# A two-layer encoder trunk on one core: seven-product matmuls over ten instead of eight of the sixteen row blocks

## The chip, the cores and the metric

The kernel runs on one core of a Trainium2 chip, as one program in one launch. The metric is device time in microseconds (us), from the first to the last work of the core; of several runs the median is taken. TensorE does the matmuls, VectorE and ScalarE the element-wise work, GpSimd some element-wise work and some DMA issue, SyncE issues most weight loads. In the profile's rows these are PE (PEld for its weight loads), DVE, ACT, POOL and SP.

## The reference, cut to what matters

256 frames of 2048 float32 features go through two layers. Layer 0 mixes with sparse attention, layer 1 with a convolution module; in both an MLP and a gated embedding follow:

```python
def sq_relu_mlp(hn, w1, w2):          # w1: 2048 x 8192, w2: 8192 x 2048
    a = jax.nn.relu(hn @ w1)
    return (a * a) @ w2
...
h = h + sq_relu_mlp(rmsnorm(h, norm_mlp_g[i]), mlp_w1[i], mlp_w2[i])
h = h + jax.nn.sigmoid(h @ ple_w_gate[i]) * (p[i] @ ple_w_proj[i])
```

The convolution of layer 1 is depthwise with 31 taps per channel. Everything is float32; the output is the normalized h.

## The kernel before

Weights stream from HBM in raw tiles of up to two row blocks (128 rows by 512 columns each, 256 KB a block). Each raw tile is split into two parts, `wh` (a ScalarE copy to the fast matmul format) and `wl` (VectorE: raw minus `wh`), and the activations are split the same way, so each block product takes three matmuls: high by high, high by low, low by high. `halves` does the split; its `wh` and `wl` tiles lie in rings of `SPLITS` buffers, and a buffer comes free when TensorE has used the tile in it.

The MLPs and the gates go through `pair_gemm`, which computes 256 frames by 1024 output columns from 2048 inputs; one call is a **pair** below. There are 36: 16 for each layer's MLP and two for each layer's gates. An MLP is done in four blocks of 2048 hidden columns, each block being four pairs: the first and the second hidden pair (**H1**, **H2**), which end in squared ReLU, transposes and a fresh split into the activations `a`; and the first and second residual pair (**R1**, **R2**), which add to `h`.

Within a pair the first `2 * SP` of the 16 row blocks go through the seven-product scheme (Strassen's, in Winograd's form): the weights of even and odd row blocks and of the two column halves form four sets `a`, `b`, `c`, `d` of `SP` blocks each, the activations are kept as sums of quarters (`Sums`), and seven products of `SP` blocks do the work of eight. `seven(m, ...)` is product m; they stand in the order 0, 5, 3, 4, 1, 6, 2. Between them the weights are summed in place: `b` is added to `a`, and later to `d`, by a DMA that accumulates (issued from GpSimd); `d` and then `c` are added to `a` on VectorE (`add`). A block of a seven-product set serves one of the two frame halves at a time, so its split feeds 3 matmuls. The other `16 - 2 * SP` row blocks are plain (`plain`): the split of a plain block feeds both frame halves, 6 matmuls.

The four results x, y, v, z gather in four PSUM banks; `taken` evicts them, early parts through ScalarE copies (hidden pairs) or VectorE adds (residual pairs), final parts through VectorE. `Sums.put` turns two transposed blocks into the sums that the seven products need (ScalarE copies, VectorE differences, two splits); plain blocks need only a split.

All raw tiles share one ring of `RAWS` = 9 tiles. Small closures are put off by steps (`defer`, `step`), and a scheduling pass of the compiler then orders each engine's instructions. Each engine takes its own in that order, and those that wait hold up what stands behind them.

The convolution's taps `wdw` are loaded and transposed (`taps`) while layer 0's attention output is projected; `wdl` holds a second, low set of taps for two channel tiles.

Of the kernel before, what the change touches and what calls it, by code (L numbers as in the profile page):

```python
# [17 lines left out]
P = 128  # L18
# [34 lines left out]
SP = 4  # L53
# [5 lines left out]
SPLITS = 6  # L59
# [3 lines left out]
def encoder(ctx: ExitStack, tc: tile.TileContext, A, inv_freq, out):  # L63
# [101 lines left out]
    class Sums:  # L165
# [19 lines left out]
        def put(self, kk, pt, g=None):  # L185

            if kk >= 2 * SP:
                h, l = (v[:, kk - 2 * SP:kk - 2 * SP + 2, :] for v in self.rest)
                put_blocks((h, l), pt, None if g is None else g[:, kk:kk + 2])
                return  # L190
            y, z, v = work(4, P), work(4, P), work(2, P)
            for k, dst in ((0, v), (1, z[:, 1:3, :])):
                nc.scalar.activation(dst, pt[:, k], AF.Copy, scale=g[:, kk + k:kk + k + 1] if g is not None else 1.0)
            x11, x21, x12, x22 = v[:, 0, :], v[:, 1, :], z[:, 1, :], z[:, 2, :]
            tt = nc.vector.tensor_tensor
            nc.vector.tensor_scalar(y[:, 0, :], x11, -1.0, None, op0=ALU.mult)
            tt(y[:, 2, :], x21, x11, op=ALU.subtract)
            tt(y[:, 3, :], x21, x22, op=ALU.subtract)
            tt(y[:, 1, :], x11, y[:, 3, :], op=ALU.subtract)
            tt(z[:, 0, :], x12, y[:, 1, :], op=ALU.subtract)  # L200
            i = kk // 2
            for dst, src in ((self.four, y), (self.more, z[:, :3, :])):
                split(dst[0][:, :, i, :], dst[1][:, :, i, :], src)
# [11 lines left out]
    def pair_gemm(x, src, taken, extras=(), apart=False):  # L215
# [13 lines left out]
        def load(ks, n):  # L229
            raw = raw_tile(len(ks))  # L230
# [21 lines left out]
        def raw(name, q):  # L252
            if (name, q) not in raws:
                raws[name, q] = load(*rows(name, q))
# [19 lines left out]
        def plain(n, ks):  # L274
            step()
            w = halves(load(ks, n))
# [17 lines left out]
        for r in ks[:-2]:  # L294
# [7 lines left out]
        plain(0, ks[-2])  # L302
# [13 lines left out]
    def raw_tile(nk, n=NB):  # L316
        return wpool.tile([P, KG, NB], F32, name="raw", tag="raw", bufs=RAWS)[:, :nk, :n]
# [472 lines left out]
    def ple(layer, x, done, e, pr, last=None):  # L790
# [3 lines left out]
        for ch in range(2):  # L794

            def projections(n, ch=ch):
                w = []

                def project(t):
                    if not w:  # L800
                        r = raw_tile(2)
# [43 lines left out]

    PE_TILES = [p[0] for p in PE_PLAN]
    wdw = const.tile([P, KT, CONV_W + 1], F32, name="wdw")
    wdl = const.tile([P, len(PE_TILES), CONV_W + 1], F32, name="wdl")

    def taps(c):  # L850
        pw = at_tile().rearrange("p (k i) -> p k i", k=KT)
        wr = work(NB)[:CONV_W]
        nc.scalar.dma_start(wr, A["b_w_dw"][0][:, c * NB:(c + 1) * NB])

        def turn():
            for k in range(4):
                nc.tensor.transpose(pw[:, k, :CONV_W], wr[:, k * P:(k + 1) * P], ident[:CONV_W, :CONV_W])
            nc.vector.tensor_copy(wdw[:, 4 * c:4 * c + 4, :CONV_W], pw[:, :4, :CONV_W])
            for i, kk in enumerate(PE_TILES):
                if kk // 4 == c:  # L860
                    wdh = small.tile([P, CONV_W + 1], F32R, name="wdh")
                    nc.scalar.activation(wdh[:, :CONV_W], wdw[:, kk, :CONV_W], AF.Copy)
                    nc.vector.tensor_tensor(wdl[:, i, :CONV_W], wdw[:, kk, :CONV_W], wdh[:, :CONV_W].bitcast(F32),
                                            op=ALU.subtract)
        defer(1, turn)
    for c in range(4):
        defer(12 + 2 * c, lambda c=c: taps(c))

# [12 lines left out]
    with tc.tile_pool(name="cnv", bufs=1) as cnv:  # L881
        u = cnv.tile([P, KT, UW], F32, name="u")
# [4 lines left out]
        class Diagonals:  # L887

            def __init__(self, kk, where):
                self.kk, self.done = kk, 0
                flat = lambda v: v.rearrange("p k s -> p (k s)").rearrange("p (i j) -> p i j", j=P)
                if where == "hl":
                    hi, lo = xpair("A")
                    m = PE_TILES.index(kk)
                    self.sets = [(flat(hi), wdw[:, kk]), (flat(lo), wdl[:, m])]
                else:
                    self.sets = [(flat(acts.tile([P, KT, S], F32, name="dg", tag=f"x{where}A")), wdw[:, kk])]
                self.some()  # L900

            def some(self, n=BUILD):
                with tc.issue_after(recent[0]):
                    for i in range(self.done, min(self.done + n, CONV_W)):
                        for d, w in self.sets:
                            nc.scalar.activation(d[:, i, :], ident, AF.Copy, scale=w[:, i:i + 1])
# [6 lines left out]
        def conv_pe(kk):  # L913
# [5 lines left out]
            if len(d.sets) == 1:  # L919
                for i in range(CONV_W):  # L920
                    nc.tensor.matmul(acc, d.sets[0][0][:, i, :], u[:, kk, i:i + S], start=i == 0, stop=i == CONV_W - 1)
            else:
                uh = cnv.tile([P, UW], F32R, name="uh")
                ul = cnv.tile([P, UW], F32R, name="ul")
                split(uh, ul, u[:, kk, :])
                hi, lo = d.sets[0][0], d.sets[1][0]
                for i in range(CONV_W):
                    nc.tensor.matmul(acc, hi[:, i, :], uh[:, i:i + S], start=i == 0, stop=False)
                    nc.tensor.matmul(acc, lo[:, i, :], uh[:, i:i + S], start=False, stop=False)
                    nc.tensor.matmul(acc, hi[:, i, :], ul[:, i:i + S], start=False, stop=i == CONV_W - 1)  # L930
# [192 lines left out]
```

## Time and profile before

| what | value |
|---|---|
| median of 3 runs | 2248.43 us (2247.61 to 2248.62) |
| profiled execution, its own time | 2248.04 us |
| its span, first to last instruction | 2246.3 us |
| mean granted TensorE clock | 0.998 |
| busy: PE, PEld, DVE, ACT, POOL | 2224.4, 1847.5, 1874.4, 1432.1, 428.6 us |
| chain that ended last, by engine | PE 93%, DVE 4%, issue 1%, DMA 1%, ACT 1% |

The span lies 1.7 us inside the profiled execution's time. Busy time is the time in which an engine has at least one instruction in flight; matmuls overlap, so the pace of TensorE is read from the starts of its matmuls and not from their durations.

### The profile page before, as it was taken

To read this page: it belongs to the slowest core of one execution; us is meant where nothing else is said; L and a number is where in the kernel's file an instruction comes from. 1 tells how busy PE (TensorE), PEld (TensorE's weight loads), DVE (VectorE), ACT (ScalarE), POOL (GpSimd) and SP (SyncE) were. 2 spreads that over 40 slices of the span, in tenths; PEclk is the share of its full clock that TensorE was granted. 3 is DMA by queue.
4 is the path that set the end of the run, shared out by engine and by line. 5 is a ranking of instruction groups with operands and counts; after the bars stand their busy time and mean duration, and the time that the engine had idled before them with its cause. 6 is when DMAs were issued, how large, how long until landed. Compare 5 with 4: busy or idle time off the path is not lost.

```text
span 2246.3 us, 29595 instructions
## 1 busy us (share of the span) xinstructions
PE 2224.4 (99%) x10366; PEld 1847.5 (82%) x10366; DVE 1874.4 (83%) x2516; ACT 1432.1 (64%) x1920; POOL 428.6 (19%) x313
## 2 busy tenths in 40 slices
PE   9999999999999999999999999999999999999998
PEld 7888778888888888888898887888888888888886
DVE  5658657988888888889868999789889889889987
ACT  6545546765765765766765744577567577577675
POOL 0201210111011011011139872111111101101012
PEclk9999999999999999999999999999999999999999
DMA  8655446887887887887767552677877877877884
GB/s 278 198 150 171 148 128 169 224 249 204 234 242 203 238 240 202 243 232 202 205 194 226 181 175 67 201 199 201 275 205 202 271 201 209 270 196 216 237 245 121
DMA packets 268021, 463.42 MB, mean 206 GB/s; under 512 B 16340, under 2 KB 62308, under 8 KB 267744
## 3 DMA queue, kind: packets, MB, share of 16 engines
q1 hardware_dynamic: 225840, 381.88, 50.9%
q0 software_dynamic: 39168, 75.51, 20.1%
q10 hardware_dynamic: 2864, 4.15, 0.6%
q8 instruction: 81, 1.33, 0.2%
q14 instruction: 68, 0.56, 0.1%
HBM read 459.38 MB, written 2.10 MB: 205 GB/s over the span
## 4 chain that ended last, share of the span: by engine, by line
PE 93%; DVE 4%; issue 1%; DMA 1%; ACT 1%; POOL 0%; SPq 0%; POOLq 0%; DVEq 0%; ACTq 0%
PE pm L238 42%; PE at L238 21%; PE pm L347 8%; PE pm L349 8%; PE pm L348 8%; PE pt L763 1%; DVE at L950 1%; PE at L808 1%; DVE wl L323 1%; PE pt L428 1%; PE at L612 0%; PE at L659 0%; PE at L689 0%; DMA work<-in_b_w_dw 0%; DMA raw<-in_a_w_in 0%
## 5 line engine op out<-in xcount | busy, mean ns | idle before, releaser
L322 ACT ACTIVATE wh<-raw 128x1024 fp32r<-128x1024 f32 (+2 forms) x1032 | 1058.8, 1040 | 621.8 <-PE at L238 187.8
L323 DVE TENSOR_TENSOR wl<-raw,wh 128x1024 fp32r<-128x1024 f32 (+1 forms) x955 | 1146.5, 1223 | 267.1 <-ACT wh L322 250.6
L261 POOL DMA_DIRECT2D raw<-in_mlp_w x128 | 155.1, 1212 | 1203.1 <-DVE wl L323 1076.3
L238 PE MATMUL pm<-wl,xhA 128*128 128x512 f32 x504 | 197.7, 392 | 0.0
L238 PE MATMUL pm<-wl,xhB 128*128 128x512 f32 x504 | 197.5, 392 | 0.0
L238 PE MATMUL pm<-wh,xlB 128*128 128x512 f32 x504 | 196.4, 391 | 0.0
L238 PE MATMUL pm<-wh,xlA 128*128 128x512 f32 x504 | 196.4, 391 | 0.0
L238 PE MATMUL pm<-wh,xhB 128*128 128x512 f32 x504 | 192.5, 392 | 0.0
L238 PE MATMUL pm<-wh,xhA 128*128 128x512 f32 x504 | 192.3, 393 | 0.0
L347 PE MATMUL pm<-wh,xhA 128*128 128x512 f32 (+2 forms) x480 | 184.1, 388 | 1.4 <-ACT xhA L382 0.6
L349 PE MATMUL pm<-wh,xlA 128*128 128x512 f32 (+2 forms) x480 | 183.6, 387 | 0.5 <-DVE xlA L1041 0.5
L348 PE MATMUL pm<-wl,xhA 128*128 128x512 f32 (+2 forms) x480 | 183.8, 384 | 0.0
L263 DVE TENSOR_TENSOR raw<-raw 128x1024 f32<-128x1024 f32 x144 | 175.5, 1220 | 1.0
L323 POOL TENSOR_TENSOR wl<-raw,wh 128x1024 fp32r<-128x1024 f32 (+1 forms) x77 | 158.3, 2079 | 30.2 <-ACT wh L322 29.1
L347 PE MATMUL pm<-wh,xhB 128*128 128x512 f32 (+1 forms) x448 | 163.1, 365 | 0.0
L348 PE MATMUL pm<-wl,xhB 128*128 128x512 f32 (+1 forms) x448 | 162.0, 362 | 0.0
L349 PE MATMUL pm<-wh,xlB 128*128 128x512 f32 (+1 forms) x448 | 161.8, 363 | 0.0
L950 DVE SCALAR_TENSOR_TENSOR at<-u,wdw,at 128x256 f32<-128x256 f32 x402 | 160.5, 483 | 0.0
L238 PE MATMUL at<-wh,xlA 128*128 128x512 f32 x360 | 140.9, 391 | 0.0
L238 PE MATMUL at<-wh,xhA 128*128 128x512 f32 x360 | 140.8, 391 | 0.0
L238 PE MATMUL at<-wh,xlB 128*128 128x512 f32 x360 | 140.8, 391 | 0.0
L238 PE MATMUL at<-wh,xhB 128*128 128x512 f32 x360 | 140.7, 391 | 0.0
(228 smaller groups left out, 3951.1 us busy)
## 6 DMA issues: line engine op xcount, KB each, us to landing
raw<-in_mlp_w SPq DMA_DIRECT2D x448, 512.0 KB, 5.4
raw<-in_mlp_w POOLq DMA_DIRECT2D x128, 512.0 KB, 6.4
raw<-in_a_w_in SPq DMA_DIRECT2D x72, 512.0 KB, 4.1
raw<-in_ple_w_gate SPq DMA_DIRECT2D x56, 512.0 KB, 5.6
raw<-in_b_w_pw SPq DMA_DIRECT2D x96, 256.0 KB, 3.1
raw<-in_a_w_out SPq DMA_DIRECT2D x32, 512.0 KB, 3.7
raw<-in_b_w_pw SPq DMA_DIRECT2D x32, 512.0 KB, 4.3
raw<-in_ple_w_gate POOLq DMA_DIRECT2D x16, 512.0 KB, 6.2
```

The source lines that it names most:

```text
L238: nc.tensor.matmul(bank[v], l, r, start=v not in begun, stop=bool(left[v] == 0 or (last and j == 2)), skip_group_check=v in again)
L261: nc.gpsimd.dma_start(r, piece(*rows(other, q)), accum_op=ALU.add)
L263: nc.vector.tensor_tensor(r, r, raw(other, q), op=ALU.add)
L322: recent[0] = nc.scalar.activation(wh, r, AF.Copy).ins
L323: (low or nc.vector).tensor_tensor(wl, r, wh.bitcast(F32), op=ALU.subtract)
L347: nc.tensor.matmul(pm[t][:, :n], a, wh[:, i], start=k + i == 0, stop=False)
L348: nc.tensor.matmul(pm[t][:, :n], a, wl[:, i], start=False, stop=False)
L349: nc.tensor.matmul(pm[t][:, :n], b, wh[:, i], start=False, stop=k + i == kt - 1)
L428: nc.tensor.transpose(pt[:, k, t, :], h[:, t, (kk + k) * P:(kk + k + 1) * P], ident)
L763: nc.tensor.transpose(pt[:, k, t, :], both[t][:, 2 * j + k, :], ident)
L808: nc.tensor.matmul(pp, l, r[:, k], start=k == 0 and j == 0, stop=k == 1 and j == 2)
L950: nc.vector.scalar_tensor_tensor(dst, src, w, z, op0=ALU.mult, op1=ALU.add)
```

## The change

`SP` goes from 4 to 5: the seven products run over ten row blocks and six stay plain. A set of five blocks is held in three raw tiles (one block, two, two) where four blocks were two tiles of two. `SPLITS` goes from 6 to 5. The one raw ring becomes three: tiles of the sets in a ring of 6 (`kept`), single-block tiles of the sets in a ring of 3 of their own, plain tiles in a ring of 3 (`used`); other matmuls take turns between the first and the last. With three plain tiles a column half in place of four, two of the first half stand before product 3 and one after product 2; the one between products 1 and 6 is gone. The sign change in `Sums.put` moves from VectorE to ScalarE where no gain is applied. The second set of taps (`wdl`) is dropped with the code that could use it, and the loading of the taps moves to the first steps of the convolution module.

```diff
-SP = 4
+SP = 5
...
-SPLITS = 6
+USED = 3
+SPLITS = 5
...
-            nc.vector.tensor_scalar(y[:, 0, :], x11, -1.0, None, op0=ALU.mult)
+            if g is None:
+                nc.scalar.activation(y[:, 0, :], pt[:, 0, 0], AF.Copy, scale=-1.0)
+            else:
+                nc.vector.tensor_scalar(y[:, 0, :], x11, -1.0, None, op0=ALU.mult)
...
-                raws[name, q] = load(*rows(name, q))
+                raws[name, q] = load(*rows(name, q), "kept")
...
-            w = halves(load(ks, n))
+            w = halves(load(ks, n, "used"))
...
-        for r in ks[:-2]:
+        for r in ks[:-1]:
             plain(0, r)
         seven(3, "z", "a", part="z1")
         add("a", "d")
...
         seven(1, "x", "a", part="x2")
         add("a", "c")
-        plain(0, ks[-2])
         seven(6, "v", "a")
         seven(2, "x", "d", part="x3")
         plain(0, ks[-1])
...
-    def raw_tile(nk, n=NB):
-        return wpool.tile([P, KG, NB], F32, name="raw", tag="raw", bufs=RAWS)[:, :nk, :n]
+    raw_turn = [0]
+
+    def raw_tile(nk, n=NB, ring=None):
+
+        if ring is None:
+            raw_turn[0] = (raw_turn[0] + 1) % 3
+            ring = "used" if raw_turn[0] == 0 else "kept"
+        if ring == "kept" and nk == 1:
+            return wpool.tile([P, 1, NB], F32, name="raw", tag="raw1", bufs=3)[:, :, :n]
+        bufs = USED if ring == "used" else RAWS - USED
+        return wpool.tile([P, KG, NB], F32, name="raw", tag=ring, bufs=bufs)[:, :nk, :n]
...
-    for c in range(4):
-        defer(12 + 2 * c, lambda c=c: taps(c))
...
     with tc.tile_pool(name="cnv", bufs=1) as cnv:
+
+        PE_TILES = [p[0] for p in PE_PLAN]
+        wdw = cnv.tile([P, KT, CONV_W + 1], F32, name="wdw")
...
+        for c in range(4):
+            defer(c, lambda c=c: taps(c))
```

How the change moves instructions is seen on VectorE, in H2 of each MLP block. The first place is the start of H2, where the results of H1 are still to be evicted. `wl` rows are splits (a 128x512 split is of a single-block tile, 128x1024 of a two-block tile), `held` rows are evictions of H1's last two banks, `work` rows the differences of `Sums.put`, `xlB` and `slB` rows its low parts. Before, from the second split of product 5 on:

```order
L323 TENSOR_TENSOR wl_5274<-raw_5271,wh_5273 128x1024
...
L200 TENSOR_TENSOR work_5115<-work_5115,work_5114 128x128
L323 TENSOR_TENSOR wl_5286<-raw_5283,wh_5285 128x1024
...
L749 TENSOR_TENSOR held_4987<-pm_4824,held_4987 128x512
L380 TENSOR_TENSOR xlB_4819<-work_5114,xhB_4817 128x4x128
L380 TENSOR_TENSOR slB_4820<-work_5115,shB_4818 128x3x128
L199 TENSOR_TENSOR work_5151<-work_5153,work_5151 128x128
L749 TENSOR_TENSOR held_4941<-at_4821,held_4941 128x512
L323 TENSOR_TENSOR wl_5304<-raw_5301,wh_5303 128x1024
```

And of the change, from the first split of product 5 on:

```order
L335 TENSOR_TENSOR wl_5369<-raw_5366,wh_5368 128x512
L761 TENSOR_TENSOR held_5106<-pm_4898,held_5106 128x512
L761 TENSOR_TENSOR held_5044<-at_4895,held_5044 128x512
L335 TENSOR_TENSOR wl_5378<-raw_5375,wh_5377 128x1024
L335 TENSOR_TENSOR wl_5390<-raw_5387,wh_5389 128x1024
...
L204 TENSOR_TENSOR work_5271<-work_5271,work_5270 128x128
L335 TENSOR_TENSOR wl_5402<-raw_5399,wh_5401 128x1024
L335 TENSOR_TENSOR wl_5420<-raw_5417,wh_5419 128x1024
L335 TENSOR_TENSOR wl_5436<-raw_5290,wh_5435 128x512
```

The two evictions, which wait for H1's last matmul, stood behind product 5 and the first plain tile (the row with raw_5283); now they stand ahead of the second and third split of product 5, and of everything behind.

The second place is later in the same pair, on VectorE between product 1 and the splits of product 6. Here `raw<-raw,raw` rows are the additions of c to a. Before, from the last split of product 1 (raw_5205) to the first of product 2 (raw_5339):

```order
L323 TENSOR_TENSOR wl_5380<-raw_5205,wh_5379 128x1024
L263 TENSOR_TENSOR raw_5193<-raw_5193,raw_5240 128x1024
L323 TENSOR_TENSOR wl_5396<-raw_5393,wh_5395 128x1024
...
L263 TENSOR_TENSOR raw_5205<-raw_5205,raw_5271 128x1024
L198 TENSOR_TENSOR work_5257<-work_5259,work_5258 128x128
L323 TENSOR_TENSOR wl_5412<-raw_5193,wh_5411 128x1024
...
L323 TENSOR_TENSOR wl_5422<-raw_5205,wh_5421 128x1024
...
L323 TENSOR_TENSOR wl_5432<-raw_5339,wh_5431 128x1024
```

And of the change, from the last split of product 1 (raw_5330) to the last of product 6:

```order
L335 TENSOR_TENSOR wl_5521<-raw_5330,wh_5520 128x1024
L204 TENSOR_TENSOR work_5317<-work_5317,work_5316 128x128
L392 TENSOR_TENSOR xlB_4893<-work_5316,xhB_4891 128x4x128
L267 TENSOR_TENSOR raw_5290<-raw_5290,raw_5366 128x512
L204 TENSOR_TENSOR work_5351<-work_5351,work_5350 128x128
L392 TENSOR_TENSOR xlB_4893<-work_5350,xhB_4891 128x4x128
L267 TENSOR_TENSOR raw_5299<-raw_5299,raw_5375 128x1024
L267 TENSOR_TENSOR raw_5330<-raw_5330,raw_5387 128x1024
L392 TENSOR_TENSOR slB_4894<-work_5317,shB_4892 128x3x128
L335 TENSOR_TENSOR wl_5536<-raw_5290,wh_5535 128x512
L392 TENSOR_TENSOR slB_4894<-work_5351,shB_4892 128x3x128
L335 TENSOR_TENSOR wl_5543<-raw_5299,wh_5542 128x1024
```

The plain tile (raw_5393) that stood between product 1 and product 6 is gone, and all three additions and the four low parts of two puts stand ahead of or among the splits of product 6; before, those low parts stood behind the splits of product 2.

## Rows read from the trace of the kernel before

**Rows 1.** The page: busy us (share of the span) xinstructions by engine.

```profile
PE 2224.4 (99%) x10366; PEld 1847.5 (82%) x10366; DVE 1874.4 (83%) x2516; ACT 1432.1 (64%) x1920; POOL 428.6 (19%) x313
```

**Rows 2.** Windows: layer 0's MLP, its gates, and one MLP block.

```profile
core 0: us, PE busy (x) PEld busy (x) DVE busy (x) ACT busy (x) POOL busy (x), PEclk, DMA share, GB/s
365.00:1033.00 668.00, 668.00 (x3023) 551.95 (x3021) 583.36 (x664) 448.77 (x547) 78.34 (x65) 1.00 0.79 220
1033.00:1120.00 87.00, 86.88 (x399) 71.21 (x398) 78.26 (x87) 62.96 (x85) 9.72 (x8) 1.00 0.79 223
...
570.00:737.00 167.00, 167.00 (x754) 138.13 (x752) 146.44 (x161) 112.06 (x133) 19.37 (x16) 1.00 0.81 226
```

**Rows 3.** The chain that ended last, in order of time: start us, us, what.

```profile
355.12 9.04 DMA work<-in_b_w_dw
...
577.57 4.99 PE pm L238 x22
```

**Rows 4.** ScalarE by line, 530:990; busy us, mean ns | idle before, its releasers.

```profile
L322 ACT ACTIVATE wh<-raw 128x1024 fp32r<-128x1024 f32 x242 | 252.0, 1058 | 133.2 <-PE at L238 62.2 <-PE pm L238 52.1 <-DVE raw L263 16.2
L750 ACT ACTIVATE held<-held,rstd 128x512 f32<-128x512 f32 x24 | 17.1, 713 | 1.6 <-DVE held L749 1.6
L751 ACT ACTIVATE held<-held 128x512 f32<-128x512 f32 x24 | 14.8, 618 | 0.1
...
L193 ACT ACTIVATE work<-pt 128x256 f32<-128x256 f32 x24 | 7.5, 380 | 3.7 <-PE pt L763 3.7
```

**Rows 5.** Timeline of VectorE, where it runs without a break: start us, us, instruction.

```profile
772.79 1.22 DVE L263 TENSOR_TENSOR raw<-raw 128x1024 f32<-128x1024 f32 x1
...
779.95 0.49 DVE L200 TENSOR_TENSOR work<-work 128x128 f32<-128x128 f32 x2
780.36 3.49 DVE L323 TENSOR_TENSOR wl<-raw,wh 128x1024 fp32r<-128x1024 f32 x3
783.76 1.29 DVE L380 TENSOR_TENSOR xlB<-work,xhB 128x512 fp32r<-128x512 f32 x2
784.97 1.02 DVE L380 TENSOR_TENSOR slB<-work,shB 128x384 fp32r<-128x384 f32 x2
785.90 4.63 DVE L323 TENSOR_TENSOR wl<-raw,wh 128x1024 fp32r<-128x1024 f32 x4
```

**Rows 6.** Timeline of TensorE: transposes of hidden results.

```profile
634.49 0.81 PE L763 MATMUL pt<-ident,held 128*128 128x128 f32 x6
...
642.66 0.27 PE L763 MATMUL pt<-ident,held 128*128 128x128 f32 x1
```

**Rows 7.** Timeline, VectorE: splits up to product 2's second tile, in H1, H2, R1, R2.

```profile
568.79 3.50 DVE L323 TENSOR_TENSOR wl<-raw,wh 128x1024 fp32r<-128x1024 f32 x3 [0.21 <-ACT wh L322]
...
613.28 3.49 DVE L323 TENSOR_TENSOR wl<-raw,wh 128x1024 fp32r<-128x1024 f32 x3
...
655.35 5.76 DVE L323 TENSOR_TENSOR wl<-raw,wh 128x1024 fp32r<-128x1024 f32 x5
...
694.68 3.49 DVE L323 TENSOR_TENSOR wl<-raw,wh 128x1024 fp32r<-128x1024 f32 x3
```

**Rows 8.** Timeline, TensorE: first matmul with that tile's low part, same four pairs.

```profile
576.27 0.39 PE L238 MATMUL at<-wl,xhA 128*128 128x512 f32 x1
...
619.49 0.39 PE L238 MATMUL at<-wl,xhA 128*128 128x512 f32 x1
...
662.42 0.39 PE L238 MATMUL at<-wl,xhB 128*128 128x512 f32 x1
...
703.00 0.39 PE L238 MATMUL at<-wl,xhB 128*128 128x512 f32 x1
```

**Rows 9.** The page: DMA queues (packets, MB, share of 16 engines' span).

```profile
q1 hardware_dynamic: 225840, 381.88, 50.9%
q0 software_dynamic: 39168, 75.51, 20.1%
```

**Rows 10.** Windows around the end of the convolution.

```profile
1372.00:1377.00 5.00, 4.08 (x20) 3.43 (x20) 3.42 (x7) 1.87 (x4) 0.69 (x1) 0.66 0.00 0
```

More of the change, by code (lines that the diff above doesn't have):

```diff
@@ L227, in piece, with load @@
             return src[:, ks.start:ks.stop:ks.step, n * NB:(n + 1) * NB]
-        def load(ks, n):
-            raw = raw_tile(len(ks))
+        def load(ks, n, ring):
+            raw = raw_tile(len(ks), ring=ring)
             nc.sync.dma_start(raw, piece(ks, n))
@@ L800, in project @@
                     if not w:
-                        r = raw_tile(2)
+                        r = raw_tile(2, ring="used")
                         nc.sync.dma_start(r, blocks(A["ple_w_proj"][layer], (2 * ch + n) * NB))
@@ L843, in ple @@
                 pair_gemm(x, src, gates(), extras)
[L846 to L865, printed above, removed]
-    for c in range(4):
-        defer(12 + 2 * c, lambda c=c: taps(c))
     with tc.tile_pool(name="sums", bufs=1) as pool:
@@ L881, in encoder, with taps, turn @@
     with tc.tile_pool(name="cnv", bufs=1) as cnv:
+        PE_TILES = [p[0] for p in PE_PLAN]
+        wdw = cnv.tile([P, KT, CONV_W + 1], F32, name="wdw")
+        def taps(c):
+            pw = at_tile().rearrange("p (k i) -> p k i", k=KT)
+            wr = work(NB)[:CONV_W]
+            nc.scalar.dma_start(wr, A["b_w_dw"][0][:, c * NB:(c + 1) * NB])
+            def turn():
+                for k in range(4):
+                    nc.tensor.transpose(pw[:, k, :CONV_W], wr[:, k * P:(k + 1) * P], ident[:CONV_W, :CONV_W])
+                nc.vector.tensor_copy(wdw[:, 4 * c:4 * c + 4, :CONV_W], pw[:, :4, :CONV_W])
+            defer(1, turn)
+        for c in range(4):
+            defer(c, lambda c=c: taps(c))
         u = cnv.tile([P, KT, UW], F32, name="u")
@@ L892, in __init__ @@
                 self.kk, self.done = kk, 0
[L893 to L899, printed above, removed]
+                self.taps = acts.tile([P, KT, S], F32, name="dg", tag=f"x{where}A").rearrange(
+                    "p k s -> p (k s)").rearrange("p (i j) -> p i j", j=P)
                 self.some()
@@ L904, in some @@
                     for i in range(self.done, min(self.done + n, CONV_W)):
[L905 to L906 removed]
+                        nc.scalar.activation(self.taps[:, i, :], ident, AF.Copy, scale=wdw[:, self.kk, i:i + 1])
                 self.done += n
@@ L918, in conv_pe @@
             acc = mm_tile()[:, :S]
[L919 to L930, printed above, removed]
+            for i in range(CONV_W):
+                nc.tensor.matmul(acc, d.taps[:, i, :], u[:, kk, i:i + S], start=i == 0, stop=i == CONV_W - 1)
             nc.scalar.activation(y[:, kk, :], acc, AF.Identity, bias=gcol["bdw"][:, kk:kk + 1])
```

## The prediction

> **What bounds the kernel now.** I read the page's busy line first: TensorE 99%, VectorE 83% [rows 1]. The windows then show where each counts: through layer 0's MLP TensorE is busy all 668.0 us, and in one MLP block of four pairs (167.0 us) TensorE has no idle time while VectorE is busy 146.4 us, 88% [rows 2]. The chain is TensorE there; its matmuls step at 4.99 / 22 = 0.227 us [rows 3]. ScalarE's high splits wait mostly for TensorE (114 of 133 us idle) to free a buffer [rows 4]: the splits run ahead until the ring is full, so TensorE is the bound. How far ahead they are when it is tightest is read from two timelines. In H1 the low split of product 2's second tile ends one step before 568.79 + 3.50 = 572.29, at 571.15, and TensorE uses it at 576.27: a reserve of 5.1 us. In H2 it ends at 615.64 (one step before 616.77) for 619.49: 3.9. In R1 at 658.84 (two steps before 661.11) for 662.42: 3.6. In R2 at 698.17 for 703.00: 4.8 [rows 7, 8]. The change eats from this reserve.
>
> **What it removes.** A pair has 3 x (64 - SP) matmuls: 180 before, 177 after; over 36 pairs 108 go, at 0.227 us [rows 3] 24.5 us, 2.7 per block of four pairs. The order view of TensorE shows that count (6480 to 6372). The second taps were read by nothing: zero.
>
> **What it adds to VectorE.** Its steps without a break are 1.135 us for 1024 columns (3.40 / 3, from 780.36 to 783.76), 0.605 for 512, 0.465 for 384 and 0.205 for 128; an addition of 1024 lasts 1.22 as a split does and is priced like one [rows 5]. A block of four pairs had 88 splits and 16 additions of 1024, 24 evictions and 8 low parts of 512, 4 of 384, and small differences of about 4 us: 143. After: 80 + 16 of 1024, 28 splits and 8 additions of 512 for the single-block tiles, 24 + 8 of 512, 5 of 384, 20 differences: 109.0 + 41.1 + 2.3 + 4.1 = 156.5 us. TensorE after: 708 x 0.227 + 32 transposes x 0.108 (the last five of six take 0.81 - 0.27 [rows 6]) = 164.2. So VectorE goes from 88% to 95%, less than TensorE over the whole block. But it is not spread evenly.
>
> **The run of products.** Each product's split feeds 3 matmuls a block, a plain one 6. From product 3 to product 2, VectorE had 10 splits, 4 additions and the plain split between products 1 and 6: 15 x 1.135 = 17.0 us, while TensorE had 72 matmuls, 16.3. After: five products at 0.605 + 2 x 1.135 = 2.9, two additions of the same, 20.1 us, against 75 matmuls, 17.0. VectorE falls behind by 3.1 where it was 0.7: 2.4 more. The ring held six tiles of two blocks, 36 matmuls, 8.2 us; five tiles of 1, 2, 2, 1, 2 blocks are 24 matmuls, 5.4 us: 2.8 less. Reserve lost: 5.2 us. That leaves H1 -0.1, H2 -1.3, R1 -1.6, R2 -0.4; a negative reserve is a wait of TensorE, in every block.
>
> **H2, from its order.** At its start the two evictions, which wait for H1's last matmul, now stand ahead of product 5's second split, and all of H1's puts but none of their cover stands before product 2's last split. All that VectorE must do from H1's last matmul until TensorE can go on with product 2's last tile is then countable in the order view: 14 splits and 4 additions of 1024 (20.4 us), 5 splits, 2 additions, 4 low parts and 2 evictions of 512 (7.9), 4 of 384 (1.9), 16 differences (3.3): 33.4 us. TensorE has 125 matmuls and 14 transposes in that stretch, 29.9. So at least 3.5 us of wait, even if VectorE never waits itself. It does: ScalarE must run a scaled ReLU (0.71), a high split (1.06), another ReLU, six copies from PSUM of up to 0.38 and a square (0.62) [rows 4] before it makes the first plain tile's high part, and an eviction before the second's; followed row by row, VectorE stands some 3 us there, and the wait is 6.6. I take 6.0, near the followed value, since the floor assumes no wait on ScalarE.
>
> **The others.** H1: -0.1 by the reserve; followed through its order 0.4; I take 0.3. R1: 1.6; in addition product 0 now needs the sum of row blocks 8 and 9, which come from H2's last results, where they were plain blocks needed later; with that chain (evict, ReLU, square, transpose, copies, differences, split) 3.8. I take 3.2. R2: 0.4; followed, product 6's last tile waits for addition, high split and low split in turn (1.14 + 1.06 + 1.22 us [rows 4, 5]) while TensorE has used what was ready: 1.8. I take 1.5. Sum per block 11.0 us of wait against 2.7 saved: +8.3, eight blocks: **+66 us**. The bounds: waits of 3.5 + 1.6 + 0.4 + 0.1 = 5.6 give +2.9 a block, +23; the followed 12.6 give +9.9, +79.
>
> The gates: their stretch of two pairs has 87.0 us and VectorE 78.3 of them [rows 2]; it gets some 4 us more a pair (the splits and additions above, and a put), 86.3, where TensorE would need 85.6. Between VectorE without idle time (-0.7) and with all of its present 8.7 (+8) I take +3.7, twice: **+7 us**.
>
> **At nothing.** The sign change on ScalarE (busy 67% of a block [rows 2]). GpSimd issues 216 accumulating DMAs for 144, and is busy 12% of a block. The taps' loading: one such load took 9.04 us on the chain before [rows 3]; now it lies in the first matmuls of the convolution and its user comes two groups of 96 matmuls later; bound 0 to 9, taken as 0, as the transposes wait only if the load is late. The five-deep ring in the plain matmuls elsewhere is still 5 x 12 matmuls, 13.6 us ahead. DMA: the accumulating queue takes 20.1% of the span for 75.5 MB, the other 50.9% for 381.9 [rows 9]; a quarter more of the first and one block of 256 KB a pair (2.5%) less of the second add 3.7% of the span, so 0.81 of a block becomes some 0.86: not the bound.
>
> **Sum.** 2248.0 (the profiled execution, 0.4 below the median) + 66 + 7 = **2321 us**, 3.2% slower. Against the median the difference is nothing here.
>
> **A page against the rows.** The Trainium skill, Perfetto Trace Analysis, Identifying the Most-Contended Engine, says to judge TensorE by the busy share of its weight loads and VectorE by occupancy, and to optimize whichever is highest. In the block these are 138.1 / 167 = 83% and 88% [rows 2]. By that rule VectorE is already the engine to relieve, and a change that loads it would lose all it adds: VectorE's 156.5 us plus its present 20.6 idle, 177 a block, +81 in all, 2336 with the gates, inside the forecast's own range. The trace disagrees for the kernel before, since TensorE's matmuls step without a gap; for the kernel after, my sum and the rule point the same way. The Trainium skill, VectorE: DVE Perf Modes, The TRN2 errata, prices an fp32 two-operand instruction at (N + 151) / 0.96 ns, 691 for 512 and 1224 for 1024, which fits the durations in the rows; with these for each of the 51 instructions of H2's stretch its floor would be 7.9 instead of 3.5. The rows show successive starts closer, so I keep 3.5.
>
> **Rivals.**
> (1) Only the floors hold, the scheduler's order hiding the rest: waits near 5.6 a block, gates 0 to +4. 2248 + 23 to 30: 2271 to 2278, with its surroundings 2253 to 2290. For it: VectorE's whole-block sum is below TensorE's. Against it: the waits on ScalarE in H2.
> (2) TensorE stays the bound, the other side: 2248 - 24.5 = 2223.5. It needs VectorE to do H2's stretch in under 29.9 us, and decides from there: either the two evictions don't hold up what is behind them, or VectorE's steps are 10% shorter than the rows'. Nothing in the trace speaks for it but the sum of the block.
> (3) Waits and savings cancel: within 4.5 us (0.2%, about what a measurement of this kernel can tell from no change), 3.1 us of wait a block, under the floor of H2 alone.
> (4) Worse: the waits pull the clock. After several waits of TensorE around the convolution's end the granted clock is 0.66 on average over 5 us [rows 10], so part of it at 1.2 GHz. One such stretch per H2, 2 us each, adds 16; loads that land late in the three separate rings could double the waits. 2365 and more.
> The change does what it says: the order view shows the 108 matmuls gone.
>
> **Chances.** Forecast (2290 to 2362) 0.63; (1) 0.22; (4) 0.06; (3) 0.05; (2) 0.04. All but (2) and (3) are slower by more than 0.2%: slower 0.91, same 0.05, faster 0.04. The range 2264 to 2358 leaves out (2), (3), (4), a third of (1) and the forecast's own last few us, together 0.2 or a little over.
>
> **What would show it.** In the profile after: TensorE's idle time in an MLP block some 11 us, ended by VectorE's splits, most of it in H2 before product 6 and product 2; VectorE busy some 156 us of a block of 175; matmuls 108 fewer at the same 0.227. It is wrong if TensorE's row shows no idle time in H2 (then VectorE's queue is not what I counted), if ScalarE or a DMA is named as the releaser instead, or if the gates or the convolution carry the difference.

## The result, and the profile after

| | before | after |
|---|---|---|
| median of 4 runs each | 2248.02 us (2247.26 to 2248.62) | 2414.91 us (2411.37 to 2420.75) |
| ratio, 95% interval | | 1.0745 (1.0721 to 1.0769) |
| profiled execution, its span | 2246.3 us | 2409.6 us |
| mean granted TensorE clock | 0.998 | 0.980 |

The change makes the kernel 7.4% slower, 167 us. The forecast said 2321, 73 us slower, with 2358 as its upper end. It had the direction, and less than half of the size.

First the page of the kernel after: busy times, then the chain that ended last, by engine and by line. It answers [rows 1] and [rows 9].

```profile
PE 2276.1 (94%) x10258; PEld 1840.7 (76%) x10258; DVE 1997.8 (83%) x2786; ACT 1496.7 (62%) x2182; POOL 495.9 (21%) x385
...
q1 hardware_dynamic: 221808, 372.45, 46.0%
q0 software_dynamic: 49536, 94.39, 24.2%
...
PE 39%; DVE 21%; issue 21%; DMA 11%; ACT 6%; POOL 1%; ACTq 0%; DVEq 0%; POOLq 0%; SPq 0%
DVE wl L335 12%; DMA raw<-in_mlp_w 9%; PE pm L359 8%; PE pm L361 8%; PE pm L360 8%; PE pm L242 7%; DVE raw L267 4%; PE at L242 4%; ACT wh L334 4%; PE pm L918 1%; DMA raw<-in_ple_w_gate 1%; POOL raw L265 1%; ACT held L762 1%; DVE xlA L392 1%; DVE xlB L392 1%
```

108 matmuls are gone, as counted. TensorE's share of the chain fell from 93% to 39%. VectorE's share was expected; 11% of DMA, nearly all of it weight loads, was not.

Second, one block of four pairs in the windows, from H1's first matmul to the next block's (the same block of the kernel before, 717.30 to 884.40, has 167.1 us, and TensorE is busy in all of them).

```profile
751.20:937.10 185.90, 173.18 (x742) 136.97 (x741) 160.30 (x191) 118.70 (x160) 27.66 (x26) 0.98 0.79 211
```

A block takes 18.8 us more. VectorE is busy for 160.3 us of 185.9, close to the 156.5 forecast, but the block was to take 175. The clock of 0.98 is new too.

Third, the waits: engine and tile waited for, total us, times, longest. These are rows of ScalarE and TensorE.

```profile
ACT wh L334 <- DMA raw<-in_mlp_w: 190.0, 56, 7.7
...
PE pm L242 <- DVE wl L335: 49.9, 50, 2.9
PE pm L242 <- DVE h L790: 23.2, 8, 3.0
PE at L242 <- DVE wl L335: 18.2, 10, 3.1
PE pm L242 <- ACT wh L334: 9.5, 14, 1.7
```

Before, ScalarE's idle time in front of high splits was ended by TensorE [rows 4]. Now 190 us of it end with a weight load. Told apart by who issued the load, 152 us (33 waits, at the end of a pair) are loads of plain tiles from SyncE and 38 us (23 waits, early in a pair) accumulating loads from GpSimd. TensorE itself still mostly names VectorE, so TensorE's own rows would not have led to the cause: ScalarE stands one engine further back in the chain load, high split, low split, matmul. The row with `h` is an eviction in R1, once in each of the eight blocks; the experiments come back to it.

Fourth, where such a load is late: the timeline at the end of H1 in the same block, for VectorE, SyncE's queue, ScalarE, VectorE and TensorE. (The last row is ScalarE at the end of H2.)

```profile
780.20 2.35 DVE L335 TENSOR_TENSOR wl<-raw,wh 128x1024 fp32r<-128x1024 f32 x2
...
782.58 0.37 SPq L235 DMA_DIRECT2D raw<-in_mlp_w  x1
...
790.19 1.06 ACT L334 ACTIVATE wh<-raw 128x1024 fp32r<-128x1024 f32 x1 [2.33 <-DMA raw<-in_mlp_w]
...
791.28 1.83 DVE L335 TENSOR_TENSOR wl<-raw,wh 128x1024 fp32r<-128x1024 f32 x2 [4.26 <-ACT wh L334]
...
791.41 0.48 PE L242 MATMUL pm<-wh,xhA 128*128 128x512 f32 x1
...
792.56 0.50 PE L242 MATMUL pm<-wl,xhA 128*128 128x512 f32 x1 [0.21 <-DVE wl L335]
...
838.60 1.06 ACT L334 ACTIVATE wh<-raw 128x1024 fp32r<-128x1024 f32 x1 [5.11 <-DMA raw<-in_mlp_w]
```

At a pair's end four plain tiles follow each other: the third of the first column half and the three of the second. Their ring has three slots, so the pair's last tile takes the slot of the one three places ahead of it. The low split of that one is the second of the two in the first row and ends at 780.20 + 2.35 = 782.55; the load is issued at 782.58; its high split starts at 790.19, 7.6 us later. TensorE comes to the tile at 791.41, and so far it has lost next to nothing. But ScalarE has stood still for 2.33 us in front of it, and the first splits of the next pair, which stand behind it in ScalarE's order, came later by that; VectorE had nothing to do for 4.26 us; and TensorE enters the next pair with no reserve (it waits 0.21 us for the low split of this tile already). At the end of H2 ScalarE loses 5.11 us in the same way.

### The profile page after: what moved, and what is told of

Same layout as the page of the kernel before. It is cut to its first block, busy times and chain, and to the rows that moved or that the text cites. A ratio compares the mean times of both kernels' runs of the same rounds, so it can differ in the third digit from the quotient of the medians.

```text
span 2409.6 us, 30357 instructions
## 1 busy us (share of the span) xinstructions
PE 2276.1 (94%) x10258; PEld 1840.7 (76%) x10258; DVE 1997.8 (83%) x2786; ACT 1496.7 (62%) x2182; POOL 495.9 (21%) x385
## 4 chain that ended last, share of the span: by engine, by line
PE 39%; DVE 21%; issue 21%; DMA 11%; ACT 6%; POOL 1%; ACTq 0%; DVEq 0%; POOLq 0%; SPq 0%
DVE wl L335 12%; DMA raw<-in_mlp_w 9%; PE pm L359 8%; PE pm L361 8%; PE pm L360 8%; PE pm L242 7%; DVE raw L267 4%; PE at L242 4%; ACT wh L334 4%; PE pm L918 1%; DMA raw<-in_ple_w_gate 1%; POOL raw L265 1%; ACT held L762 1%; DVE xlA L392 1%; DVE xlB L392 1%
## 5 line engine op out<-in xcount | busy, mean ns | idle before, releaser
L334 ACT ACTIVATE wh<-raw 128x1024 fp32r<-128x1024 f32 (+2 forms) x1212 | 1111.8, 954 | 685.2 <-DMA raw<-in_mlp_w 190.0
L335 DVE TENSOR_TENSOR wl<-raw,wh 128x1024 fp32r<-128x1024 f32 (+2 forms) x1135 | 1211.8, 1107 | 288.8 <-ACT wh L334 277.1
L265 POOL DMA_DIRECT2D raw<-in_mlp_w x192 | 212.8, 1122 | 1305.1 <-DVE wl L335 1121.2
L267 DVE TENSOR_TENSOR raw<-raw 128x1024 f32<-128x1024 f32 (+1 forms) x216 | 224.4, 1050 | 0.5
L242 PE MATMUL pm<-wh,xlB 128*128 128x512 f32 x414 | 159.2, 390 | 0.0
L242 PE MATMUL pm<-wh,xlA 128*128 128x512 f32 x414 | 159.2, 390 | 0.0
L242 PE MATMUL at<-wl,xhB 128*128 128x512 f32 x378 | 149.7, 396 | 9.3 <-DVE wl L335 9.3
L242 PE MATMUL at<-wl,xhA 128*128 128x512 f32 x378 | 149.3, 395 | 8.9 <-DVE wl L335 8.9
L242 PE MATMUL pm<-wh,xhB 128*128 128x512 f32 x414 | 153.6, 393 | 2.4 <-ACT wh L334 2.4
L242 PE MATMUL pm<-wh,xhA 128*128 128x512 f32 x414 | 153.4, 392 | 0.7 <-ACT wh L334 0.7
```

The lines of the kernel that those rows point to most:

```text
L242: nc.tensor.matmul(bank[v], l, r, start=v not in begun, stop=bool(left[v] == 0 or (last and j == 2)), skip_group_check=v in again)
L265: nc.gpsimd.dma_start(r, piece(*rows(other, q)), accum_op=ALU.add)
L267: nc.vector.tensor_tensor(r, r, raw(other, q), op=ALU.add)
L334: recent[0] = nc.scalar.activation(wh, r, AF.Copy).ins
L335: (low or nc.vector).tensor_tensor(wl, r, wh.bitcast(F32), op=ALU.subtract)
```

## The experiments

Two theories. **A**: the three-deep ring of plain tiles, which the forecast's sum has no term for, adds the missing 90 us or so. **B**: VectorE's run of products, the forecast's mechanism, costs the whole, and the late load fills time that would be lost anyway. A third, **C**, for the ring of splits, which went from six tiles to five.

**The last plain tile into the other ring** (`e1_kept_last`).

```diff
-        def plain(n, ks):
+        def plain(n, ks, ring="used"):
...
-            w = halves(load(ks, n, "used"))
+            w = halves(load(ks, n, ring))
...
-            plain(1, r)
+            plain(1, r, "kept" if r is ks[-1] else "used")
```

> The changed kernel, with one edit: the last plain tile of each pair is loaded into the six-deep ring of the sets instead of the three-deep ring of plain tiles, so that its load need not wait for the low split of the plain tile three places ahead of it. Theory A (the three-deep plain ring costs what lies between the forecast and the result, some 90 us): 2300 to 2340 us, ScalarE's idle time ended by weight loads falls from 190 us to under 60, and what is left is the forecast's wait on VectorE. Theory B (VectorE's run of products alone costs the whole, and the late load only fills time that would be lost anyway): 2390 to 2415 us, with the wait now ended by VectorE.

Measured: 2360.82 us (2359.32 to 2364.28), 1.0504 of before (1.0489 to 1.0520), 54 us under the kernel after. ScalarE's row for weight loads in this kernel, and a block in the windows:

```profile
ACT wh L334 <- DMA raw<-in_mlp_w: 4.2, 4, 2.1
```

```profile
738.70:916.60 177.90, 169.84 (x742) 136.93 (x741) 159.23 (x190) 119.91 (x160) 26.52 (x25) 0.98 0.81 219
```

190.0 us became 4.2, and a block 185.9 became 177.9. So the late load is a cause of its own, as A has it, but 54 us and not 90: both theories missed the number. The edit has a cost of its own, too: at the last gates TensorE waits 5.6 us for the load of `p`, which it does not in the kernel after. In the two MLPs alone the edit brings 57 us (1495.1 to 1438.1). What is left there can be held against the forecast's own terms. TensorE in H2 of this block:

```profile
805.91 0.51 PE L242 MATMUL pm<-wh,shA 128*128 128x512 f32 x1 [0.48 <-ACT wh L334]
809.31 0.80 PE L242 MATMUL pm<-wl,shA 128*128 128x512 f32 x1 [2.90 <-DVE wl L335]
809.90 0.63 PE L242 MATMUL pm<-wh,slA 128*128 128x512 f32 x1
810.33 0.63 PE L242 MATMUL pm<-wh,shA 128*128 128x512 f32 x1
810.76 0.63 PE L242 MATMUL at<-wh,xhA 128*128 128x512 f32 x1
```

The longest wait of the block stands before the low part of product 6's first tile, where the forecast put it: VectorE works without a break there, and two additions and a low part of a put stand ahead of that split. I add up the steps between starts of successive matmuls in this block, less the 0.222 us of a full-speed step and less what the same pairs have before: H1 0.6, H2 5.6, R1 3.0, R2 1.8 us. The last two starts show something else: the step is 0.43 us where it was 0.227 [rows 3]. The granted clock of 809.90 to 814.60 is 0.50, that is 1.2 instead of 2.4 GHz. In this block 13 matmuls run so, 13 x 0.21 = 2.7 us. 11.0 + 2.7 less 2.7 us of saved matmuls is 11.0, against 177.9 - 167.1 = 10.8 measured.

R1's wait stands elsewhere than the forecast had it. VectorE and TensorE in R1 of this block:

```profile
844.08 1.22 DVE L267 TENSOR_TENSOR raw<-raw 128x1024 f32<-128x1024 f32 x1
845.21 0.68 DVE L335 TENSOR_TENSOR wl<-raw,wh 128x512 fp32r<-128x512 f32 x1
845.81 1.22 DVE L267 TENSOR_TENSOR raw<-raw 128x1024 f32<-128x1024 f32 x1
846.95 2.35 DVE L335 TENSOR_TENSOR wl<-raw,wh 128x1024 fp32r<-128x1024 f32 x2
849.22 0.68 DVE L790 TENSOR_TENSOR h<-h,pm 128x512 f32<-128x512 f32 x1
...
849.95 0.50 PE L242 MATMUL pm<-wh,shB 128*128 128x512 f32 x1 [2.57 <-DVE h L790]
```

TensorE is at product 4's first matmul, which goes on in the bank of product 3; that bank must first be evicted, in a residual pair by an add on VectorE, and this add stands behind additions and splits. It is the same in all eight blocks, 2.57 us each, and the 23.2 us of `h` in the kernel after are the same place.

**The additions left out**, without and with the edit above (`e2_no_add`, `e5_kept_noadd`), and half of them (`e9_no_add_c`, which has the edit above).

```diff
-                    nc.vector.tensor_tensor(r, r, raw(other, q), op=ALU.add)
+                    raw(other, q)
```

> The changed kernel without VectorE's additions of c and d to a (that part of the computation is left out), which takes about 5.75 us of VectorE's work out of every pair, more than the change added, and leaves the rings as they are. Theory A: the late load of each pair's last plain tile stays, so only the forecast's part goes: 2330 to 2370 us, and ScalarE still has over 120 us of idle time ended by weight loads. Theory B (VectorE is the whole cause): TensorE becomes the bound again, 2225 to 2260 us.

> Both edits at once: the last plain tile of each pair in the six-deep ring (as in e1_kept_last), and VectorE's additions of c and d to a left out (as in e2_no_add; that part of the computation is left out). If the late load of the last plain tile and VectorE's run of products are all there is, each hides part of the other (54 us and 86 us came back one at a time, 140 of the 191 us that lie above 2248.0 less the 24.5 us of saved matmuls), and with both gone TensorE is the bound: 2222 to 2245 us, the granted clock back at 0.99 or more. If a third cause holds the rest (the ring of five splits, GpSimd's late accumulating loads, the gates): 2260 to 2290 us.

> e1_kept_last with only the addition of c to a left out on VectorE (that part of the computation is left out): 2.9 us a pair, half of what e5_kept_noadd takes off and somewhat less than the 3.4 us a pair that the change added to VectorE. If waits come from a reserve that runs out (VectorE's added work against the ring of splits, as the forecast has it), most of them go with the first half: 2265 to 2300 us. If each addition costs its own length wherever it stands (linear between 2361 and 2259): about 2310 us. If the order of H2 and ScalarE hold TensorE and not VectorE's work: over 2330 us.

Measured: 2325.22 us in one run, 2258.86 us (2257.15 to 2260.53), and 2316.3 us in one run. As a table, with the bound that all matmuls saved and no wait would give, 2248.0 - 24.5 = 2223.5:

| us | additions made | left out | difference |
|---|---|---|---|
| ring as changed | 2414.9 | 2325.2 | 89.7 |
| last plain tile in the other ring | 2360.8 | 2258.9 | 101.9 |
| difference | 54.1 | 66.3 | |

Of the 191.4 us above the bound, the ring is 54 to 66, VectorE's additions 90 to 102, and 35.4 is neither. The parts add up without much overlap, so B's second half, that the late load is hidden by VectorE's lateness, is out. In `e2_no_add` the loads are still late:

```profile
ACT wh L334 <- DMA raw<-in_mlp_w: 228.3, 82, 6.4
```

Of these 228 us, 134 are SyncE's loads at the ends of pairs, in 33 waits as in the kernel after (152 us there); the other 94 are GpSimd's accumulating loads. The column of VectorE's additions is to be read with care: leaving them out takes 5.75 us off a pair, where the change added 3.4, and it also removes the high split's wait for the sum and frees the tiles of c earlier. So 90 to 102 us is what the additions cost in this kernel, and not what the added work costs.

Both of my numbers for `e2_no_add` were off: 2325 lies 5 us under A's range and far over B's. `e5_kept_noadd` missed its first range by 14 us and came in at the lower edge of the second. Its block:

```profile
715.70:882.90 167.20, 165.25 (x741) 135.68 (x740) 137.30 (x166) 119.20 (x160) 26.49 (x24) 1.00 0.89 233
```

Even with 22 us of VectorE's work taken out of a block (159.2 less 137.3), and the clock whole, a block takes as long as before (167.2 against 167.1), not 2.7 less. The same count of steps gives 0.6, 1.3, 0.1 and 1.0 us of waits. Half of the additions brought 44.5 us of the 102, so the linear guess (2310) was nearest and the reserve guess (2265 to 2300) failed: H2's waits fell from 5.6 to 2.3 us, but R1 kept its 3.0. VectorE and TensorE there:

```profile
829.80 2.35 DVE L269 TENSOR_TENSOR raw<-raw 128x1024 f32<-128x1024 f32 x2
832.07 1.82 DVE L337 TENSOR_TENSOR wl<-raw,wh 128x1024 fp32r<-128x1024 f32 x2
...
830.73 0.39 PE L242 MATMUL at<-wh,xhB 128*128 128x512 f32 x1
833.95 0.79 PE L242 MATMUL at<-wl,xhB 128*128 128x512 f32 x1 [2.83 <-DVE wl L337]
834.54 0.63 PE L242 MATMUL at<-wh,xlB 128*128 128x512 f32 x1
...
835.39 0.63 PE L242 MATMUL pm<-wh,shB 128*128 128x512 f32 x1
```

TensorE waits for the low split of product 1's first tile, the second of the two in VectorE's second row; in this kernel the compiler has put that matmul ahead of product 4 (the last row), whose first two low splits ended at 828.75 and 829.88. TensorE takes its instructions in order and waits. The tile's high part was ready at 830.20, but VectorE, without a break, first ran two additions of d and another split. So it is an order on both engines: the additions of d stand ahead of the split, `e9_no_add_c` leaves them in, and without them (`e5_kept_noadd`) R1 waits 0.1.

**More and less of the rings.** Two slots for plain tiles instead of three (`e8_used2`); the three rings in the kernel before (`e3_rings`); five splits in the kernel before (`e4_splits5`); four in `e1_kept_last` (`e11_splits4`).

```diff
-RAWS = 9
-USED = 3
+RAWS = 8
+USED = 2
```

> The changed kernel with two slots in the ring of plain tiles instead of three (a dose more of the suspected cost). The last plain tile but one then reuses the slot that is split shortly before it, and the last one that of the tile two ahead of it, two plain tiles or 5.3 us of matmuls before TensorE needs it, while a load takes 6 to 8 us from issue to the first split. Theory A (late loads of plain tiles are a cause of their own): 2470 to 2650 us, with ScalarE's idle time ended by weight loads more than doubled from 190 us. Theory B (those waits lie beside VectorE's lateness and cost nothing of their own): under 2430 us.

```diff
-        def load(ks, n):
-            raw = raw_tile(len(ks))
+        def load(ks, n, ring):
+            raw = raw_tile(len(ks), ring=ring)
```

> The kernel before, with its one raw ring of nine replaced by the three rings of the change (six, three, three); eight row blocks stay in the seven products and the ring of splits stays at six. With four plain tiles a column half, the last two tiles of each pair now reuse slots that are split shortly before. Theory A: the loads come late as in the changed kernel, 2290 to 2350 us (some 2 us a pair or more lost after the reserve of 3.6 to 5.1 us is used up), with ScalarE's idle time ended by weight loads over 100 us. Theory B: the rings cost nothing by themselves, 2245 to 2253 us.

```diff
-SPLITS = 6
+SPLITS = 5
```

> The kernel before with the ring of splits at five tiles instead of six, and nothing else. The forecast took 2.8 us off a reserve of 3.6 to 5.1 us, which leaves TensorE without a wait: 2246 to 2256 us. Theory C (the shorter ring of splits is a main cause by itself): over 2275 us, with TensorE waiting for low splits in every block. Theory A has nothing here: 2246 to 2256 us.

```diff
-SPLITS = 5
+SPLITS = 4
```

> e1_kept_last with the ring of splits at four tiles instead of five: another 2.7 us or so less of matmuls that the splits can be ahead. By the forecast's reserve, which fell by 2.8 us with the sixth tile and is already used up at five, each pair of a block waits up to 2.8 us more: 8 x 4 x 1.5 to 2.8 = 50 to 90 us on top of 2361, 2410 to 2450 us. If the ring of splits no longer matters at ten row blocks (only VectorE's sum of work does): 2355 to 2375 us.

Measured: 2449.92 us in one run; 2287.35 us, 1.0181 (1.0164 to 1.0198); 2259.59 us, 1.0052 (1.0037 to 1.0067); 2401.59 us in one run. With two slots the kernel loses 35 us more, less than A's 55 to 235 and more than B's 15: ScalarE's waits for weight loads in the MLPs did not double (167.7 us), but the lateness now reaches TensorE itself, whose waits for high splits were 9.5 us:

```profile
PE pm L242 <- ACT wh L334: 43.4, 33, 2.8
```

The rings alone, in the kernel before, cost 39.6 us (26 in the MLPs, 12 from the last gates on), and its ScalarE shows the same row:

```profile
ACT wh L332 <- DMA raw<-in_mlp_w: 221.6, 83, 7.2
```

So the ring does its harm without the two further row blocks; of 2290 to 2350 expected, the low end. Five splits alone cost 11.8 us, 3.6 us over the forecast's upper end and under half of C's price: a block takes 168.3 us against 167.1, and by the steps it is H2 that waits, where the reserve of 3.9 less 2.8 should have covered it. A further tile off the ring, at ten row blocks, costs 40.8 us in a single run, a little under the 50 to 90 expected (and part of it may be late loads again, for which ScalarE waits 52 us there against 4.2):

```profile
747.50:930.70 183.20, 171.99 (x741) 135.91 (x740) 160.86 (x190) 121.59 (x160) 26.44 (x25) 0.99 0.79 212
```

**The work put elsewhere.** The low splits of the last three plain tiles on GpSimd (`e6_pool`), those of the seven single-block tiles (`e7_pool1`), and the addition of c as an accumulating DMA (`e10_dma_c`), all on top of `e1_kept_last`.

```diff
-            w = halves(load(ks, n, ring))
+            w = halves(load(ks, n, ring), nc.gpsimd if n else None)
```

> e1_kept_last with the low splits of each pair's last three plain tiles on GpSimd instead of VectorE, which takes 3 x 1.135 = 3.4 us of VectorE's work out of a pair, 13.6 a block, where 12 to 13 us a block are waited for. If VectorE's work is what TensorE waits for in e1_kept_last, and GpSimd's splits (2.4 us each, against 2.7 us of matmuls on such a tile) come in time: 2250 to 2300 us. If GpSimd's order stands against it (its accumulating loads come late behind these splits): 2340 us or more, with waits on GpSimd or on accumulated tiles.

```diff
-                w = halves(raw(name, q))
+                w = halves(raw(name, q), nc.gpsimd if len(q) == 1 else None)
```

> e1_kept_last with the low splits of the seven single-block tiles of each pair on GpSimd: 7 x 0.605 = 4.2 us a pair off VectorE, 17 a block, where 12 to 13 us a block are waited for; it takes them out of the run of products itself. If the forecast is right that VectorE's run of products is what is late: 2240 to 2300 us. If GpSimd, which takes 1.29 us for each and has its accumulating loads among them, is late in its turn: 2340 us or more, with TensorE's waits ended by GpSimd's splits.

```diff
-                if other == "b":
+                if other in "bc":
...
-        seven(6, "v", "a")
         seven(2, "x", "d", part="x3")
         plain(0, ks[-1])
+        seven(6, "v", "a")
```

> e1_kept_last with c added to a by an accumulating DMA from GpSimd instead of by VectorE, and product 2 and the plain tile that follows it put ahead of product 6, so that 15 + 12 matmuls (6 us) cover the addition, which takes some 8 us to land. All of the computation is done. VectorE is relieved as in e9_no_add_c; the accumulating queue takes half as much again (24% of the span becomes some 36%, the DMA share of a block 0.79 becomes 0.9). If VectorE's work is the cause and the DMA has room: 2290 to 2330 us. If the accumulating loads come late: over 2360 us, with waits of the high splits on these loads.

Measured: 2368.47 us, 1.0533 (1.0517 to 1.0549); 2472.81 us, 1.0995 (1.0977 to 1.1014); 2499.72 us, 1.1120 (1.1092 to 1.1147). None helps, two do much harm, and my favoured ranges failed in all three. In `e6_pool` twelve splits left VectorE in a block, 13.6 us of work, but its busy time fell by 2.7 only (5.7 in the block ahead of it):

```profile
737.80:916.20 178.40, 170.60 (x741) 137.29 (x740) 156.53 (x178) 119.89 (x160) 60.05 (x37) 0.98 0.84 218
```

What stayed on VectorE became longer; the last section shows how. In `e7_pool1` a block has 28 splits less on VectorE, and VectorE is busy for 160.6 us, no less than the 159.2 of `e1_kept_last`. GpSimd is also late in its turn, and TensorE names it:

```profile
PE pm L242 <- POOL wl L335: 42.1, 9, 5.2
PE at L242 <- POOL wl L335: 35.3, 17, 6.7
```

In `e10_dma_c` the accumulating loads are late (DMA share of a block 0.91), and the high splits wait for them (240 of these 251 us are GpSimd's loads):

```profile
ACT wh L334 <- DMA raw<-in_mlp_w: 251.0, 136, 4.2
```

**The rest of the change alone** (`e12_rest`): eight row blocks, one ring, six splits, but the taps and the sign change as after.

```diff
-            nc.vector.tensor_scalar(y[:, 0, :], x11, -1.0, None, op0=ALU.mult)
+            if g is None:
+                nc.scalar.activation(y[:, 0, :], pt[:, 0, 0], AF.Copy, scale=-1.0)
+            else:
+                nc.vector.tensor_scalar(y[:, 0, :], x11, -1.0, None, op0=ALU.mult)
...
-    for c in range(4):
-        defer(12 + 2 * c, lambda c=c: taps(c))
...
+        for c in range(4):
+            defer(c, lambda c=c: taps(c))
```

> The kernel before with the rest of the change alone: the second set of taps dropped, the loading of the taps moved to the first steps of the convolution, and the sign change on ScalarE; eight row blocks in the seven products, one raw ring, six splits. The forecast put all of this at nothing, with a bound of 9 us for the taps: 2246 to 2250 us. If the taps' load comes late where it now lies: 2252 to 2258 us, with the wait at the convolution's first matmuls.

Measured: 2246.84 us, 0.9996 (0.9987 to 1.0005). It costs nothing.

## Why the prediction was right and wrong

**What bounds the kernel before, and what goes**: right. TensorE was the bound, and 108 matmuls went; no experiment that computes everything turned them into time.

**What it adds to VectorE**: right. 156.5 us of a block forecast, 159.2 to 160.3 measured.

**The run of products, H2 from its order, the others**: right in size, and in H2 right in the mechanism too; seen without disturbance only once the ring is mended. Forecast H1 0.3, H2 6.0, R1 3.2, R2 1.5, together 11.0 us; measured in `e1_kept_last` 0.6, 5.6, 3.0, 1.8, together 11.0. In the kernel after, the same count gives 3.0, 7.6, 4.7, 2.8, together 18.1: each pair begins without its reserve. The agreement in R1 is partly luck: the forecast had 1.6 us there from the reserve at product 2 and the rest from product 0's late sum, but no wait stands in product 0, and 2.57 us of the 3.0 stand at product 4, for an eviction behind VectorE's additions and splits, which is in no term. In R2 the longer wait, 0.75 us, stands before product 1 and not product 6. And the reserve read from one tile per pair was too generous, as `e4_splits5` shows.

**The step that failed**: "At nothing", and with it the sum. The list there names the rings of splits and the DMA's share, and the ring of three plain tiles is in no term. Its mechanism stood in rival (4) ("loads that land late in the three separate rings could double the waits"), with no working and, together with the clock, 6 chances in 100. It measured 54 to 66 us. With that mended, 40 us of the 94 between forecast and result are left, past the forecast's upper end still; they are mostly the clock and the ends, below. The ring could have been worked out beforehand: the order of plain tiles and three slots give which tile reuses which, hence 24 matmuls of cover and a rest, against a load and two splits in sequence. I asked of DMA only whether its share was full (0.79 after, where 0.86 was forecast, so it was not) and never when a slot came free.

**The clock**: rival (4) has 16 us for it and the forecast none. What the low clock takes away, if TensorE has work throughout, is (1 - clock) x span: 0.020 x 2409.6 = 48 us after, 0.015 x 2362.5 = 35 in `e1_kept_last`, 0.002 x 2246.3 = 4.5 before. That is an upper bound, since waits lie in these stretches too. Counted by matmuls that began at a granted clock of 0.50 in the MLPs, there are 178 after, 96 in `e1_kept_last` and none before; at 0.21 us each that is 37 and 20 us. It comes mostly with waits in H2, as rival (4) has it, but it needs no worse case: the forecast's own waits bring it.

**The gates and the ends of layers**: +7 forecast. In the kernel after, from the first matmul of the last gates to the end takes 115.8 us against 106.1, and the first layer's first gate pair 51.5 against 49.4, together 11.8. The last residual pair of a layer, not treated apart, takes 48.4 against 42.7, twice: another 11 us at nothing in the forecast.

**Rivals**: (1), (2) and (3) are out. (4), with 2365 and more, has the time and names both the late loads and the clock, without the sizes. **The Trainium skill**, Perfetto Trace Analysis, Identifying the Most-Contended Engine: the rule as the forecast worked it out gave 2336, with VectorE losing all it adds, and came 15 us nearer than the forecast. In `e1_kept_last` a block of 177.9 us has VectorE busy for 159.2 and idle for 18.7, where the rule gave 156.5 and 20.6, so there the number agrees with it. In the kernel after it missed for the same reason as the forecast: a ring is no engine.

For `e1_kept_last` the sum of the MLPs closes: its eight blocks are 94 us longer than before, against 8 x 8.3 = 66 of forecast waits, 96 matmuls at half clock, 20, and 11 at the ends of layers, 97 together. From the last gates to the end it takes 125.3 us against 106.1, 19 more, where the forecast has +7 for all gates; 5.6 of these are the wait for `p`, the rest was not taken apart. What stays open as well is part of the 35 us that `e5_kept_noadd` has left: 3 us of waits a block and 9 us from the last gates on (115.4 against 106.1; 3.0 of them the wait for `p`) are seen there, their causes were not tried one by one. Six splits with ten row blocks were not tried. No version here is faster than the kernel before.

## What to carry to other kernels

When one ring of buffers is divided, write down for each ring which tile reuses whose slot, and compare the work between that slot's release and the new tile's use with a load's time from issue to first use; a full total of buffers says nothing about it. A producer that stands still at the end of one stage takes the reserve away from the next, so look one and two engines behind the one that waits. When TensorE is the bound and is made to wait, add the matmuls that it then runs at the lower clock to the price: here 20 us on 66 us of waits less saved matmuls.

## What the runs showed of the hardware

**GpSimd and VectorE hold each other up.** VectorE's splits in one block, of `e1_kept_last` and then of `e6_pool` (count, busy us, mean ns):

```profile
L335 DVE TENSOR_TENSOR wl<-raw,wh 128x1024 fp32r<-128x1024 f32 x80 | 95.1, 1219 | 14.3 <-ACT wh L334 13.0 <-PE pm L242 0.7 <-DMA raw<-in_mlp_w 0.4
```

```profile
L335 DVE TENSOR_TENSOR wl<-raw,wh 128x1024 fp32r<-128x1024 f32 x69 | 89.8, 1320 | 12.0 <-ACT wh L334 11.5
```

And one pair of instructions in `e7_pool1`, GpSimd's and VectorE's:

```profile
816.98 1.30 POOL L335 TENSOR_TENSOR wl<-raw,wh 128x512 fp32r<-128x512 f32 x1 [9.20 <-ACT wh L334]
...
817.04 1.78 DVE L392 TENSOR_TENSOR xlB<-work,xhB 128x512 fp32r<-128x512 f32 x1
```

VectorE's low part, 0.68 us elsewhere in this stretch, starts 0.06 us after GpSimd's split and takes 1.78: the 1.1 us more are about what the split still had to run (1.24). It seems to go the other way as well: GpSimd's splits of 1024 columns take 2.83 us on average in this block of `e6_pool`, and 2.40 in the kernel after, though there they stand in other stages. The Trainium skill, SBUF — State Buffer, SBUF: two separate sides, says that a VectorE operation with two inputs in SBUF and a GpSimd operation that reads SBUF lock a shared pair of ports, and that the later one blocks for the whole of the other; these rows agree.

**The clock fell around waits of some 3 us, and not each time.** Windows of the kernel after: a wait in H2, and a stretch that begins 1.5 us after its end:

```profile
822.10:825.52 3.42, 0.50 (x1) 0.18 (x1) 3.42 (x6) 2.93 (x5) 0.00 (x0) 1.00 0.98 211
827.01:830.42 3.41, 3.29 (x8) 2.62 (x9) 3.41 (x5) 1.71 (x3) 0.00 (x0) 0.50 1.02 352
```

Eight matmuls in 3.41 us is half the usual pace, and the granted clock is 0.50. In H2 of `e1_kept_last`, shown above, the stretch at 0.50 begins at 807.89, inside the wait that ends at 809.31. In `e9_no_add_c` the same wait of 3.0 us in R1 is followed by 8 slow matmuls in one block, 14 in the next and none in the third, and R1 takes 46.6, 47.8 and 45.0 us.
